# Meta-token keys as a full 128-row tile, and the output products of an RWKV chunk ordered by array tile

## The chip, the cores and the metric

The kernel runs on one core of one Trainium2 chip. The metric is the time of one execution on the device in microseconds (us). TensorE is called PE here, its weight loads PEld; VectorE is DVE, ScalarE is ACT, GpSimd is POOL, SyncE is SP. "Granted clock" is the share of TensorE's full speed (2.4 GHz) that the records show; it is either 1.0 or 0.5 (1.2 GHz) at any moment.

## The reference, cut to what matters

A one-layer decoder trunk over 1024 tokens with 16 learned "meta" tokens in front (1040 positions). One projection feeds four mixers; their outputs are concatenated, projected and normalised, and a mixture of 16 experts follows. The change touches three of the mixers' parts:

```python
# A: sliding window, 4 heads: the keys are the 16 meta tokens, the block before, the own block
kpos = jnp.concatenate([meta positions 0..15, qpos - BLOCK, qpos], axis=1)
p = jax.nn.softmax(jnp.concatenate([s, sink], axis=-1), axis=-1)[..., :-1]
o = jnp.einsum('bnhgqk,bnkhd->bnqhgd', p, vw)
# B: differential attention, 4 heads, causal over all earlier positions (meta tokens too)
attn = p[:, :, 0] - lam * p[:, :, 1]
o = jnp.einsum('bhqk,bkhd->bqhd', attn, vp)
# C: RWKV-7, a state S of 64x64 per head, 4 heads, 1040 steps
S = S * w_t + sa * (kk_t * a_t) + v_t * k_t        # outer products
y_t = S @ r_t
```

Meta tokens are dropped from the output, so attention is computed for 8 blocks of 128 queries. Blocks of keys begin at position 16, and the 16 meta keys stand alone in front.

## The kernel before, in words

The whole kernel is one program in float32 (some products as pairs of float32r halves). After a stage for the input norm and the first projections (to about 320 us of the profile), one long stage holds the rest of the projections, the RWKV recurrence and both attentions (about 320 to 735 us); then come the output projection with norm and routing (to about 900 us) and the experts.

In the long stage nothing is ordered by hand. Each piece of work is a step, `add(engine, cost, function, deps, priority, take, use)`, with an estimated cost in us; `Steps.run` (line 145) takes, again and again, the step that could start first by these estimates (ties by priority), and calls its function, which writes the instructions. The order in which the steps are called is the order of each engine's queue; an engine works through its queue strictly in that order. `take` and `use` stand for slots in rings of buffers (two PSUM tiles "tp", two score tiles "sc", two tiles "at" and so on).

RWKV is cut into 17 chunks of 64 positions (one pad chunk part). `chain(i)` (line 1038) holds the serial part. For each chunk: `f1` (state times input, L1056), `g1` (L1079), `h1` (new state, L1095), and `y1` (L1112 to 1116), which makes the chunk's outputs: for 2 tiles of channels `ct` and 2 halves `par` it adds two products into the same 64x64 piece of PSUM, one of the old state with a 64x64 array tile (`w.s0[q, ct]`, L1115) and one of 128 rows with a 128x64 array tile (`o.bz[:, par, 1, j]`, L1116). A float32 product is two instructions, so `y1` is 16 instructions. It runs for chunks 1 to 16. `y2` copies the result out on ACT.

The value rows live in `vs` (9 blocks of 128 rows, three groups of 128 columns); block 0 holds the 16 meta rows in partitions 0 to 15, its other partitions are never written or read. `values` (L1259) loads and transposes them; `switch` (L1234) closes the projections' buffers and opens the pool in which `vs` lies.

Sliding-window attention, `swa(kv, i)` (L1339), runs 2 x 8 times, each for two heads `g`: scores, minimum, exponential, transposes of the probabilities of the near blocks (`t1`, L1383), of the 16 meta columns (`t3`, L1391), copies to `at` (ACT L1386; DVE L1394), then the products `p1`: for each `g` the near blocks (L1403, 128 rows) and the meta block (L1404, 16 rows). Differential attention, `diff(h, i)` (L1423), runs 4 x 8 times: the key blocks stand in the order 1 to i+1, then 0, in groups of four; each group is transposed (`t1`, L1522), the full blocks are copied by ACT (`t2`, L1525), the 16-row meta block by DVE (`t3`, L1528); then `p1` multiplies the full blocks (L1542) and the meta block (L1543). `p2_` (L1407, L1546) scales the result out of PSUM.

Of the kernel before, what the change touches and what calls it, by code (L numbers as in the profile page):

```python
# [13 lines left out]
AF = mybir.ActivationFunctionType  # L14
# [5 lines left out]
P = 128  # L20
# [4 lines left out]
M = 16  # L25
NT = S + M
C = 64
# [167 lines left out]
def build(tc, A, out, dbg=None, upto=99):  # L195
# [62 lines left out]
    add = sA.add  # L258
# [10 lines left out]
    o = 0  # L269
# [531 lines left out]
    small = {}  # L801
# [236 lines left out]
    def chain(i):  # L1038
        o = grp[i]
        add = st_.add  # L1040
        p2 = lambda t: t.rearrange("p (a c) -> p a c", c=C)
        for ci, c in enumerate(o.chunks):
            pr = PRG(i)
            four = [(ct, par, HALF[par], HALF[1 - par], ct * o.nc + ci) for ct in range(2) for par in range(2)]
            w = O()
            _, sdone, sslot = state
            rd = None
            sps_dep = []
            if c > 0:
                ss_, sr, sp_ = Slot("ca"), Slot("r"), Slot("sp0")  # L1050

                def f1(w=w, ci=ci, four=four):
                    w.s0 = state[0]
                    w.r = rt("r", [2, C])
                    for ct, par, q, r, j in four:
                        T.matmul(small["ca"][q, ct * C:(ct + 1) * C], o.ab[q, ct, ci, 0], w.s0[q, ct], start=True, stop=True)  # L1056

                def f2(w=w, ci=ci):
                    V.tensor_tensor(w.r, p2(small["ca"]), o.lv[:, :, ci], op=ALU.add)

                def f3(w=w, c=c):
                    w.sp0 = rt("sp0", [2, C])
                    for ct in range(2):
                        G.tensor_scalar(w.sp0[:, ct], w.s0[:, ct], pend[:, ct, c:c + 1], None, op0=ALU.mult)
                a = add("PE", .25, f1, [sdone, o.loaded], pr, take=[ss_, sr], use=[sslot, o.slot])
                rd = add("DVE", dve(P), f2, [a, o.lvd], pr, use=[ss_, sr, o.slv])
                if c < NCH - 1:
                    sps_dep = [add("Pool", 2 * pol(C), f3, [a], pr, take=[sp_], use=[sslot])]
            else:
                sr = o.slv  # L1070

                def f2(w=w, ci=ci):
                    w.r = o.lv[:, :, ci]
                rd = add("DVE", 0, f2, [o.lvd], pr)
            scs = Slot("cs")

            def g1(w=w, four=four):
                for ct, par, q, r, j in four:
                    T.matmul(small["cs"][q, ct * C:(ct + 1) * C], o.X[q, j], w.r[q, ct], start=True, stop=True)  # L1079

            def g2(ci=ci):
                ACT.activation(o.bz[HALF[0], 0, 1, ci::o.nc], p2(small["cs"])[HALF[0]], AF.Copy)

            def g3(ci=ci):
                V.tensor_copy(o.bz[HALF[1], 1, 1, ci::o.nc], p2(small["cs"])[HALF[1]])
            a = add("PE", .25, g1, [rd, o.Xd], pr, take=[scs], use=[sr, o.sX])
            sad = [add("ACT", act(P), g2, [a] + o.bzd, pr, use=[scs, o.sbz]), add("DVE", dve(P), g3, [a] + o.bzd, pr, use=[scs, o.sbz])]
            s0slot = sslot
            if c < NCH - 1:
                sh, ns = Slot("cp"), Slot("s1")  # L1090

                def h1(w=w, four=four):
                    w.s1 = rt("s1", [2, C])
                    for ct, par, q, r, j in four:
                        T.matmul(small["cp"][q, ct * C:(ct + 1) * C], o.bz[:, par, 0, j], o.bz[:, par, 1, j], start=True, stop=True)  # L1095

                def h2(w=w, c=c):
                    s1_ = w.s1
                    for ct in range(2):
                        d, pe_ = small["cp"][:, ct * C:(ct + 1) * C], pend[:, ct, c:c + 1]  # L1100
                        if c > 0:
                            V.scalar_tensor_tensor(s1_[:, ct], d, pe_, w.sp0[:, ct], op0=ALU.mult, op1=ALU.add)
                        else:
                            V.tensor_scalar(s1_[:, ct], d, pe_, None, op0=ALU.mult)
                    state[0] = s1_
                a = add("PE", .43, h1, sad, pr, take=[sh, ns], use=[o.sbz])
                state[1] = add("DVE", 2 * dve(C), h2, [a] + sps_dep, pr, use=[sh, ns] + ([sp_] if c > 0 else []))
                state[2] = ns
            if c > 0:
                sy = Slot("cy")  # L1110

                def y1(w=w, ci=ci, four=four):  # L1112
                    for ct, par, q, r, j in four:
                        d = small["cy"][q, ct * C:(ct + 1) * C]
                        T.matmul(d, w.s0[q, ct], o.ab[q, ct, ci, 1], start=True, stop=False)  # L1115
                        T.matmul(d, o.bz[:, par, 1, j], o.gs[:, par, j, C:2 * C], start=False, stop=True)  # L1116

                def y2(c=c):
                    ACT.activation(MX[:, 4:6, (c - 1) * C:c * C], p2(small["cy"]), AF.Copy)
                a = add("PE", .7, y1, sad, pr + .05, take=[sy], use=[s0slot, o.slot, o.sbz, o.sgs])  # L1120
                ydone[c] = add("ACT", act(P), y2, [a], pr + .05, use=[sy])
# [137 lines left out]
    def values(i, pr, deps):  # L1259
# [8 lines left out]
        for j0 in (0, 4, 8):  # L1268
            j1 = min(j0 + 4, 9)
            lo = max(j0, 1)  # L1270
            sl = Slot("tp")
            v = O()

            def t1(v=v, j0=j0, j1=j1):
                v.tb = bank2("tp")
                for j in range(j0, j1):
                    a, n = (0, M) if j == 0 else (M + P * (j - 1), P)
                    T.transpose(v.tb[:n, (j - j0) * P:(j - j0 + 1) * P], w.t[:, 0, a:a + n], ident)

            def t2(v=v, j0=j0, j1=j1, lo=lo):  # L1280
                ACT.activation(vs[:, lo:j1, i * P:(i + 1) * P],
                               v.tb.rearrange("p (a c) -> p a c", c=P)[:, lo - j0:j1 - j0], AF.Copy)
                if j0 == 0:
                    ACT.activation(vs[:M, 0, i * P:(i + 1) * P], v.tb[:M, :P], AF.Copy)
            a = st_.add("PE", .45, t1, [l], pr, take=[sl], use=[se])
            out.append(st_.add("ACT", act(512), t2, [a], pr, use=[sl]))
# [52 lines left out]
    def swa(kv, i, pr, tabs, vals):  # L1339
# [48 lines left out]
        def t3():  # L1388
            w.tm = bank2("tp")
            for g in range(2):  # L1390
                T.transpose(w.tm[:M, g * P:(g + 1) * P], w.E[:, g, 0:M], ident)  # L1391

        def t4():
            V.tensor_copy(fl(w.at[:M, 4:6]), w.tm[:M, :2 * P])  # L1394

        def p1():
            w.po = bank2("tp")
# [2 lines left out]
            for g in range(2):  # L1400
                o = w.po[:, P * g:P * g + P]
                for z in range(n):
                    T.matmul(o, w.at[:, g * n + z], vs[:, i + 1 if n == 1 else i + z, vc], start=(z == 0), stop=False)  # L1403
                T.matmul(o, w.at[:M, 4 + g], vs[:M, 0, vc], start=False, stop=True)  # L1404

        def p2_():
            V.tensor_tensor(out_tile(kv)[:, i].rearrange("p (a b) -> p a b", b=64), w.po[:, :2 * P].rearrange("p (a b) -> p a b", b=P)[:, :, 64 * kv:64 * kv + 64],  # L1407
# [15 lines left out]
    def diff(h, i, pr, tabs, vals):  # L1423
# [81 lines left out]
            cb = add("Pool", 2 * pol(W), c3, [r], pr, use=[sE])  # L1505
        else:
            cb = add("DVE", dve(W), c2, [r], pr, use=[sE])
        blocks = list(range(1, i + 2)) + [0]
        last = []
        for b0 in range(0, len(blocks), 4):  # L1510
            bl = blocks[b0:b0 + 4]
            full = [j for j in bl if j]
            stt = Slot("tp")
            v = O()

            def t1(v=v, bl=bl, b0=b0):
# [1 line left out]
                if b0 == 0:  # L1518
                    w.at = at_("at", [9, P])
                for z, j in enumerate(bl):  # L1520
                    a_, n_ = (M + P * (j - 1), P) if j else (0, M)
                    T.transpose(v.tb[:n_, z * P:(z + 1) * P], w.E[:, 0, a_:a_ + n_], ident)  # L1522

            def t2(v=v, full=full):
                ACT.activation(fl(w.at[:, full[0]:full[-1] + 1]), v.tb[:, :len(full) * P], AF.Copy)  # L1525

            def t3(v=v, z=len(bl) - 1):
                V.tensor_copy(w.at[:M, 0], v.tb[:M, z * P:(z + 1) * P])  # L1528
            a = add("PE", .11 * len(bl), t1, [cb], pr, take=[stt] + ([] if b0 else [sat]), use=[sE] + ([sat] if b0 else []))
            inorder("t", a)  # L1530
            if full:
                last.append(add("ACT", act(128 * len(full)), t2, [a], pr, use=[stt, sat]))
            if 0 in bl:
                last.append(add("DVE", dve(128), t3, [a] + last[:1], pr, use=[stt, sat]))

        def p1():
            w.po = bank2("tp")
            out_tile(2 + hp_)
            o = w.po[:, :P]
            vc = slice(P + P * hp_, 2 * P + P * hp_)  # L1540
            for j in range(1, i + 2):
                T.matmul(o, w.at[:, j], vs[:, j, vc], start=(j == 1), stop=False)  # L1542
            T.matmul(o, w.at[:M, 0], vs[:M, 0, vc], start=False, stop=True)  # L1543

        def p2_():
            ACT.activation(out_tile(2 + hp_)[:, i, 64 * hh_:64 * hh_ + 64], w.po[:, 64 * hh_:64 * hh_ + 64], AF.Copy, scale=w.rs[:, 0:1])  # L1546
# [59 lines left out]
    for ct in range(2):  # L1606
# [3 lines left out]
        for q, w in enumerate(cw_):  # L1610
            conv_silu(ct, q, w, last)
    sw = [st_.add("SY", 0, switch, sp_, 0)]
    load_qk(0, sw)
    tabs = [st_.add("SY", 6, tables, after, 30)]
    tabs = [st_.add("DVE", 1.6, far_bias, tabs, 5)]
# [796 lines left out]
```

## Time and profile before

| what | value |
|---|---|
| median of 3 runs | 1461.32 us (1460.78 to 1466.42) |
| the profiled execution: its time, its span | 1463.69 us, 1461.8 us |
| mean granted TensorE clock | 0.908 |
| PE busy, share of the span | 1286.5 us, 88% |
| DVE busy | 913.9 us, 63% |
| ACT busy | 623.7 us, 43% |
| POOL busy | 279.2 us, 19% |

The page counts an engine as busy while any of its instructions runs; matmuls are pipelined, so a busy PE may still be slow at what it does. How long a matmul really holds PE is read from the time between the starts of neighbours in the timeline, not from its own duration. The span is divided into stretches by what runs in them, and each stretch has its own limit.

### The profile page before, as it was taken

The numbers are of one execution on the slowest core, as the hardware profiler recorded it, in microseconds if no ns is written. First come the engines' busy times: TensorE is split into PE (matmuls) and PEld (weight loads), VectorE is DVE, ScalarE is ACT, GpSimd is POOL, SyncE is SP. The second block draws the span as 40 slices with busy tenths as digits, with TensorE's granted clock in tenths as the row PEclk, the third lists the DMA queues.
The fourth block names the chain that finished last, engine by engine and source line by source line (L and its number), as shares of the span: only waits on it lengthen the run. The fifth ranks groups of instructions, "written<-read, shape, count | busy, mean of one in ns | idle before, by whom it ended". The sixth has DMA issues, their size and how long they took to land. (4 is left out here: it accounts for less than half of the span.)

```text
span 1461.8 us, 22362 instructions
## 1 busy us (share of the span) xinstructions
PE 1286.5 (88%) x8095; PEld 1041.1 (71%) x8095; DVE 913.9 (63%) x1713; ACT 623.7 (43%) x1101; POOL 279.2 (19%) x252
## 2 busy tenths in 40 slices
PE   5998899999989999889879986799899899889960
PEld 4896898887767688767557765677677678677750
DVE  7556649983234657557468776747754882875275
ACT  6353212233133445336643224636643771764151
POOL 3522213331102022132100113111121211111100
PEclk9999999999957989959779996999999999999995
DMA  8214337221360220400143265978966994996452
GB/s 200 78 45 134 128 106 213 86 74 59 77 162 19 69 69 21 98 23 1 58 135 138 101 182 186 298 238 245 350 183 186 357 338 137 278 335 174 138 175 116
DMA packets 165465, 219.65 MB, mean 150 GB/s; under 512 B 36046, under 2 KB 134490, under 8 KB 165036
## 3 DMA queue, kind: packets, MB, share of 16 engines
q1 hardware_dynamic: 156604, 188.66, 40.5%
q0 software_dynamic: 8688, 28.87, 8.2%
q8 instruction: 86, 1.41, 0.4%
q14 instruction: 87, 0.71, 0.1%
HBM read 174.38 MB, written 45.46 MB: 150 GB/s over the span
## 5 line engine op out<-in xcount | busy, mean ns | idle before, releaser
L454 PE MATMUL acc<-hh,wh 128*128 128x256 f32 (+2 forms) x288 | 97.1, 338 | 0.0
L454 PE MATMUL acc<-hh,wl 128*128 128x256 f32 (+2 forms) x288 | 93.2, 325 | 0.0
L2124 PE MATMUL rw<-wh,at 128*128 128x512 f32 x224 | 83.8, 424 | 8.4 <-ACT at L2099 5.8
L1180 DVE SCALAR_TENSOR_TENSOR CY<-MX,cvw,CY 128x1024 f32<-128x1024 f32 x60 | 87.9, 1485 | 0.1
L454 PE MATMUL acc<-hl,wh 128*128 128x256 f32 (+2 forms) x288 | 87.7, 323 | 0.0
L1668 DVE TENSOR_TENSOR wl<-MX,wh 128x1024 fp32r<-128x1024 f32 x66 | 78.4, 1221 | 12.1 <-ACT wh L1664 9.4
L2128 POOL DMA_INDIRECT acc__132<-y,ixs x21 | 40.9, 1948 | 183.8 <-issue 58.7
L1668 DVE TENSOR_TENSOR wol<-MX,woh 128x1024 fp32r<-128x1024 f32 x51 | 60.8, 1222 | 18.5 <-ACT woh L1664 12.3
L1664 ACT ACTIVATE wh<-MX 128x1024 fp32r<-128x1024 f32 x66 | 66.8, 1051 | 9.4 <-DMA MX<-in_exp_w_dram 6.9
L1478 ACT ACTIVATE E<-sc,nm 128x144 f32<-128x144 f32 (+7 forms) x64 | 47.9, 750 | 42.4 <-DVE nm L1472 31.2
L454 PEld LDWEIGHTS acc<-hh,wh 128*128 128x128 f32 x288 | 55.6, 193 | 5.7 <-issue 5.2
L1502 POOL TENSOR_TENSOR E<-E,rho 128x272 f32<-128x272 f32 (+3 forms) x16 | 20.8, 1298 | 197.9 <-DVE rho L1496 118.4
L2124 PEld LDWEIGHTS rw<-wh,at 128*128 128x128 f32 x224 | 44.0, 198 | 19.8 <-ACT at L2099 6.7
L1826 PE MATMUL oacc<-woh,mh 128*128 128x512 f32 x128 | 55.1, 430 | 1.8 <-ACT woh L1778 1.7
L1664 ACT ACTIVATE woh<-MX 128x1024 fp32r<-128x1024 f32 x51 | 51.9, 1050 | 10.4 <-DMA MX<-in_exp_w_dram 7.1
L454 PEld LDWEIGHTS acc<-hh,wl 128*128 128x128 f32 x288 | 55.3, 192 | 1.3 <-issue 1.0
L2100 DVE TENSOR_TENSOR xte<-acc,xte 128x512 fp32r<-128x512 f32 x44 | 28.6, 686 | 40.4 <-ACT xte L2099 40.4
L1826 PE MATMUL oacc<-wol,mh 128*128 128x512 f32 x128 | 52.3, 408 | 1.5 <-DVE wol L1781 1.5
L454 PEld LDWEIGHTS acc<-hl,wh 128*128 128x128 f32 x288 | 53.6, 189 | 0.0
L1826 PE MATMUL oacc<-woh,ml 128*128 128x512 f32 x128 | 52.0, 406 | 0.0
L2119 DVE TENSOR_TENSOR act<-act,acc 128x256 f32<-128x256 f32 x31 | 13.0, 421 | 57.9 <-ACT act L2118 57.0
L2099 ACT ACTIVATE xte<-acc 128x512 fp32r<-128x512 f32 x44 | 24.3, 596 | 57.1 <-PE acc L2097 26.1
(474 smaller groups left out, 3576.2 us busy)
## 6 DMA issues: line engine op xcount, KB each, us to landing
MX<-in_exp_w_dram SPq DMA_DIRECT2D x192, 256.0 KB
MX<-in_exp_w_dram SPq DMA_DIRECT2D x48, 512.0 KB
CY<-in_exp_w_dram SPq DMA_DIRECT2D x64, 256.0 KB
raw<-in_w_in_dram SPq DMA_DIRECT2D x20, 512.0 KB
qk<-dqk SPq DMA_DIRECT2D x64, 130.0 KB
CY<-in_exp_w_dram SPq DMA_DIRECT2D x16, 512.0 KB
dab<-ab SPq DMA_DIRECT2D x2, 2176.0 KB
qk<-dqk SPq DMA_DIRECT2D x16, 260.0 KB
```

The lines of the kernel that those rows point to most:

```text
L454: T.matmul(v.acc[:, :wid], wt[:, k], x[:, k, c0:c0 + wid], start=(z + y == 0 and wt is w.h), stop=(z + y == len(ks) - 1))
L1180: V.scalar_tensor_tensor(y, hc[:, M + j:M + j + S], cvw[:, ct, j:j + 1], y, op0=ALU.mult, op1=ALU.add)
L1478: ACT.activation(w.E[:, c, off:W], w.sc[c][:, :W - off], AF.Exp, bias=w.nm[:, c:c + 1], scale=-1.0, accum_out=w.s[:, c:c + 1])
L1502: G.tensor_tensor(w.E[:, 1, :W], w.E[:, 1, :W], w.rho.to_broadcast([P, W]), op=ALU.mult)
L1664: ACT.activation(slot_h[i % HLS][0], raw[i], AF.Copy)
L1668: eng.tensor_tensor(l, raw[i], h.bitcast(F32), op=ALU.subtract)
L1826: T.matmul(v.o, x_[:, k], y_[k][:, 512 * n:512 * n + 512], start=(i == 0 and j == 0), stop=False)
L2099: ACT.activation(dst[:, 0, s], tb[:, :m * P], AF.Copy)
L2100: V.tensor_tensor(dst[:, 1, s], tb[:, :m * P], dst[:, 0, s].bitcast(F32), op=ALU.subtract)
L2119: V.tensor_tensor(s, s, a[:, 256:512], op=ALU.mult)
L2124: T.matmul(o[n], at[:, x, k * P:(k + 1) * P], w[k][y][:, n * 512:n * 512 + 512], start=(k == 0 and (x, y) == (0, 0)), stop=(k == 3 and x = ...
L2128: G.indirect_dma_start(out=acc_, out_offset=bass.IndirectOffsetOnAxis(ap=ix[:, 0:1], axis=0), in_=y, in_offset=None, compute_op=ALU.add)
```

## The change

Three edits, one idea in each.

1. The meta keys are treated like any other block of 128 keys. The transposes take columns 0 to 127 of the scores in place of 0 to 15, all 128 rows are copied to `at`, and the products run over 128 rows of `vs[:, 0]`. One new DVE step, after `switch`, sets `vs[:, 0]` to zero, so that rows 16 to 127 (which hold probabilities of keys 0 to 111 of block 1) add nothing.
2. In `diff` the block order becomes 0 to i+1. The DVE copy `t3` goes; ACT's `t2` copies all blocks of a group. The number of groups is the same as before; for i = 3 and 7 the last group is one full block copied by ACT, where it was the meta block copied by DVE.
3. In `y1` the eight products are reordered: the two 128x64 ones of `ct` 0, then the two 64x64 ones of `ct` 0, the two 64x64 ones of `ct` 1, and the two 128x64 ones of `ct` 1.

```diff
@@ chain, y1
-                    for ct, par, q, r, j in four:
-                        d = small["cy"][q, ct * C:(ct + 1) * C]
-                        T.matmul(d, w.s0[q, ct], o.ab[q, ct, ci, 1], start=True, stop=False)
-                        T.matmul(d, o.bz[:, par, 1, j], o.gs[:, par, j, C:2 * C], start=False, stop=True)
+                    for ct in range(2):
+                        for k in (ct, 1 - ct):
+                            for _, par, q, r, j in four[2 * ct:2 * ct + 2]:
+                                d = small["cy"][q, ct * C:(ct + 1) * C]
+                                if k:
+                                    T.matmul(d, w.s0[q, ct], o.ab[q, ct, ci, 1], start=(k == ct), stop=(k != ct))
+                                else:
+                                    T.matmul(d, o.bz[:, par, 1, j], o.gs[:, par, j, C:2 * C], start=(k == ct), stop=(k != ct))
@@ swa
-                T.transpose(w.tm[:M, g * P:(g + 1) * P], w.E[:, g, 0:M], ident)
+                T.transpose(w.tm[:, g * P:(g + 1) * P], w.E[:, g, 0:P], ident)
-            V.tensor_copy(fl(w.at[:M, 4:6]), w.tm[:M, :2 * P])
+            V.tensor_copy(fl(w.at[:, 4:6]), w.tm[:, :2 * P])
-                T.matmul(o, w.at[:M, 4 + g], vs[:M, 0, vc], start=False, stop=True)
+                T.matmul(o, w.at[:, 4 + g], vs[:, 0, vc], start=False, stop=True)
@@ diff
-        blocks = list(range(1, i + 2)) + [0]
+        blocks = list(range(i + 2))
-            def t2(v=v, full=full):
-                ACT.activation(fl(w.at[:, full[0]:full[-1] + 1]), v.tb[:, :len(full) * P], AF.Copy)
-            def t3(v=v, z=len(bl) - 1):
-                V.tensor_copy(w.at[:M, 0], v.tb[:M, z * P:(z + 1) * P])
+            def t2(v=v, bl=bl):
+                ACT.activation(fl(w.at[:, bl[0]:bl[-1] + 1]), v.tb[:, :len(bl) * P], AF.Copy)
-            if full:
-                last.append(add("ACT", act(128 * len(full)), t2, [a], pr, use=[stt, sat]))
-            if 0 in bl:
-                last.append(add("DVE", dve(128), t3, [a] + last[:1], pr, use=[stt, sat]))
+            last.append(add("ACT", act(128 * len(bl)), t2, [a], pr, use=[stt, sat]))
-            for j in range(1, i + 2):
-                T.matmul(o, w.at[:, j], vs[:, j, vc], start=(j == 1), stop=False)
-            T.matmul(o, w.at[:M, 0], vs[:M, 0, vc], start=False, stop=True)
+            for j in blocks:
+                T.matmul(o, w.at[:, j], vs[:, j, vc], start=(j == 0), stop=(j == blocks[-1]))
@@ after switch
+    sw.append(st_.add("DVE", .3, lambda: V.memset(vs[:, 0], 0.0), sw, 0.5))
```

## Rows read from the trace of the kernel before

**Rows 1.** Page, part 1: busy time of each engine

```profile
PE 1286.5 (88%) x8095; PEld 1041.1 (71%) x8095; DVE 913.9 (63%) x1713; ACT 623.7 (43%) x1101; POOL 279.2 (19%) x252
```

**Rows 2.** Windows: stretch, length, busy us of PE, PEld, DVE, ACT, POOL, clock, DMA

```profile
320.00:394.00 74.00, 72.12 (x760) 59.01 (x759) 28.42 (x62) 19.43 (x37) 12.96 (x14) 1.00 0.15 50
394.00:422.00 28.00, 23.80 (x205) 18.34 (x207) 6.10 (x21) 9.62 (x28) 3.15 (x6) 0.64 0.94 233
422.00:735.00 313.00, 289.67 (x2466) 224.61 (x2463) 183.23 (x587) 146.53 (x388) 63.65 (x60) 0.84 0.18 45
735.00:900.00 165.00, 139.21 (x668) 106.05 (x667) 122.87 (x326) 55.36 (x79) 20.76 (x20) 0.86 0.45 149
```

**Rows 3.** Waits of PE, 422 to 735 us: total, times, longest

```profile
PE prep L993 <- DVE um L1017: 7.1, 3, 3.7
PE tp L1542 <- DVE at L1528: 2.1, 2, 1.7
```

**Rows 4.** Timeline of PE, full clock: start, us, line, out<-in, array tile, operands

```profile
586.02 0.45 PE L1056 MATMUL chain<-s,abv 64*64 64x64 f32 x8
586.40 0.66 PE L1522 MATMUL tp<-c__63,E 128*128 128x128 f32 x4
...
588.87 0.45 PE L1095 MATMUL chain<-bz 128*64 128x64 f32 x8
589.25 0.33 PE L1115 MATMUL chain<-abv,s 64*64 64x64 f32 x2
589.51 0.33 PE L1116 MATMUL chain<-gs,bz 128*64 128x64 f32 x2
...
591.31 0.73 PE L1460 MATMUL sc<-qk,qk 128*128 128x512 f32 x2
```

**Rows 5.** Timeline of PE at half clock, the same work

```profile
637.33 0.70 PE L1095 MATMUL chain<-bz 128*64 128x64 f32 x8 [0.60 <-DVE bz L1085]
637.96 0.47 PE L1115 MATMUL chain<-abv,s 64*64 64x64 f32 x2
...
641.18 0.69 PE L983 MATMUL prep<-c__63,abv 64*128 64x64 f32 x4
```

**Rows 6.** Windows of line L1116 alone: stretch, length, PE, PEld, clock, DMA

```profile
320.00:394.00 74.00, 5.26 (x32) 3.06 (x32) 1.00 0.15 50
394.00:422.00 28.00, 3.21 (x16) 1.91 (x16) 0.64 0.94 233
422.00:735.00 313.00, 15.94 (x80) 9.45 (x80) 0.84 0.18 45
```

**Rows 7.** Timeline of PE, full clock, attention products and a meta transpose

```profile
488.36 0.61 PE L1403 MATMUL tp<-vs,at 128*128 128x128 f32 x4
...
490.36 0.66 PE L1522 MATMUL tp<-c__63,E 128*128 128x128 f32 x4
...
493.90 1.28 PE L1542 MATMUL tp<-vs,at 128*128 128x128 f32 x10
495.11 0.48 PE L1543 MATMUL tp<-vs,at 16*128 16x128 f32 x2
495.53 0.68 PE L993 MATMUL prep<-X,um 64*64 64x64 f32 x16
496.14 0.39 PE L1391 MATMUL tp<-c__63,Es 128*16 128x128 f32 x2
496.36 0.60 PE L1522 MATMUL tp<-c__63,E 128*128 128x128 f32 x4
```

**Rows 8.** Groups by line, 420 to 735 us: count | busy us, mean ns | idle before

```profile
L1543 PE MATMUL tp<-vs,at 16*128 16x128 f32 x64 | 16.7, 343 | 0.0
...
L1528 DVE COPY at<-tp 16x128 f32<-16x128 f32 x32 | 8.8, 274 | 5.7 <-ACT at L1525 3.9 <-PE tp L1522 1.8
```

**Rows 9.** Groups by line and shape, ACT, 422 to 735 us

```profile
L1525 ACT ACTIVATE at<-tp 128x128 f32<-128x128 f32 x8 | 2.2, 273 | 2.6 <-PE tp L1522 2.5
```

**Rows 10.** Timeline of PE at the switch to attention

```profile
408.64 1.86 PE L1278 MATMUL tp<-c__63,E 128*16 128x128 f32 x8 [1.64 <-DMA E<-dvv]
```

More of the change, by code (lines that the diff above doesn't have):

```diff
@@ L1276, in t1 @@
                 for j in range(j0, j1):
-                    a, n = (0, M) if j == 0 else (M + P * (j - 1), P)
+                    a, n = (0, P) if j == 0 else (M + P * (j - 1), P)
                     T.transpose(v.tb[:n, (j - j0) * P:(j - j0 + 1) * P], w.t[:, 0, a:a + n], ident)
@@ L1511, in diff @@
             bl = blocks[b0:b0 + 4]
-            full = [j for j in bl if j]
             stt = Slot("tp")
@@ L1520, in t1 @@
                 for z, j in enumerate(bl):
-                    a_, n_ = (M + P * (j - 1), P) if j else (0, M)
-                    T.transpose(v.tb[:n_, z * P:(z + 1) * P], w.E[:, 0, a_:a_ + n_], ident)
-            def t2(v=v, full=full):
-                ACT.activation(fl(w.at[:, full[0]:full[-1] + 1]), v.tb[:, :len(full) * P], AF.Copy)
-            def t3(v=v, z=len(bl) - 1):
-                V.tensor_copy(w.at[:M, 0], v.tb[:M, z * P:(z + 1) * P])
+                    a_ = M + P * (j - 1) if j else 0
+                    T.transpose(v.tb[:, z * P:(z + 1) * P], w.E[:, 0, a_:a_ + P], ident)
+            def t2(v=v, bl=bl):
+                ACT.activation(fl(w.at[:, bl[0]:bl[-1] + 1]), v.tb[:, :len(bl) * P], AF.Copy)
             a = add("PE", .11 * len(bl), t1, [cb], pr, take=[stt] + ([] if b0 else [sat]), use=[sE] + ([sat] if b0 else []))
             inorder("t", a)
-            if full:
-                last.append(add("ACT", act(128 * len(full)), t2, [a], pr, use=[stt, sat]))
-            if 0 in bl:
-                last.append(add("DVE", dve(128), t3, [a] + last[:1], pr, use=[stt, sat]))
+            last.append(add("ACT", act(128 * len(bl)), t2, [a], pr, use=[stt, sat]))
         def p1():
```

## Prediction

> **What bounds the kernel now.** I read the page first: PE is busy 88% of the span, the next engine, DVE, 63% [rows 1]. That is an average over stages, so I cut the span into stretches. The edits touch only work between 320 and 735 us, and there PE is busy 72 of 74, 24 of 28 and 290 of 313 us, while DVE has 183 and ACT 147 of the last 313 [rows 2]. So PE bounds the stretch; what ends its idle time is read next, and it is little: the 23 us of idle from 422 to 735 are scattered, the largest single cause is 7.1 us in 3 waits [rows 3]. The middle stretch, 394 to 422, is different: DMA is at 0.94 of its engines, DVE works 6 of 28 us [rows 2], and PE waits for the value loads [rows 10]. Busy does not mean well used: the timeline shows how far apart PE's instructions start, and that is what the change alters. The granted clock is at its lower level for part of the stage (mean 0.84 from 422 on, 1.00 before 394 [rows 2]).
>
> **The change part by part.**
>
> **RWKV's outputs.** At full clock one y1 holds PE from 589.25 to 591.31: 2.06 us for 16 instructions, as eight pairs of 0.26 that alternate between a 64x64 and a 128x64 array tile [rows 4]. The same kinds of product, eight in a row on one kind of tile and going back and forth between its two halves, take 0.38 us with the step to the next kind: L1095 for the 128x64 kind (588.87 to 589.25), L1056 for the 64x64 kind (586.02 to 586.40) [rows 4]. So a pair in a row costs 0.095 and a pair in alternation 0.26; 0.16 is then the most that a change of tile can cost. The new order is four 128x64 instructions, eight 64x64, four 128x64: two such bursts, 0.76, plus one more change, 0.16, in all 0.92. It saves 1.14 us per chunk. At half clock the same rows give 3.22 us for y1 (637.96 to 641.18) and 0.63 for the burst of eight (637.33 to 637.96) [rows 5]; a pair alternating is 0.40, in a row 0.16, so the new order takes 1.26 + 0.24 = 1.50 and saves 1.72.
> Where the 16 chunks lie: 8 instructions of L1116 each, so 32, 16 and 80 records are 4, 2 and 10 chunks [rows 6]. The first four run at full clock: 4.6 us. The last ten take 0.199 us busy per record, against 0.164 in the first four and 0.200 in the middle two, where both levels of clock occur [rows 6]; I take half of the ten at each level: 14.3 us. The middle two would save 2.9 us, but PE there waits for the value loads afterwards [rows 10], so it would only wait longer; I count nothing.
>
> **Products over the meta block.** A sliding-window p1 holds PE from 488.36 to 490.36, 2.00 us for 12 instructions, four of them on 16 rows [rows 7]. Twelve ordinary ones cost 12 times 0.11 to 0.12: ten of L1542 take 1.21 us (493.90 to 495.11), and that already holds the step to the 16-row tile [rows 7]. New time 1.32 to 1.45, saving 0.55 to 0.68; over 16 tasks 9 to 11 us. A differential p1 goes from 493.90 to 495.53, 1.63 for 12, so 0.18 to 0.31 is saved where the next instruction changes the tile anyway (here a 64x64 burst); 32 tasks, as 64 records of L1543 show [rows 8], give 6 to 10. Where a full tile follows, the sliding-window rows say more (0.3 per pair), so I take the upper ends: 20 us together, all after 422.
> A rule speaks against this term. The Trainium skill, page "TensorE: Matmul & The Clock Gate", section "Why this matters for your kernels", says that a single product over 32 rows takes as long as one over 128, and gains only when several run at once. By it the 16-row pairs would cost no more than full ones and the 20 us would be nothing; the rows disagree, since the 16-row pair with its way out takes 0.42 (495.11 to 495.53) where two ordinary ones take 0.24 [rows 7]. I sum by the rows, and keep the rule as a rival.
>
> **Transposes and copies.** The 16-column transposes become 128 columns wide. A pair of them starts 0.22 us before its follower (496.14 to 496.36), 0.11 each, no less than full instructions [rows 7], so I count 0 and at most 0.05 each on 67 of them, 3 us, as the other end. DVE loses 32 copies of 0.274, 8.8 us [rows 8]. ACT gets them as wider copies; a copy of 128 columns alone is 0.273 [rows 9], so at most 8.7 us, on an engine that idles for more than half of the stretch. Two PE waits of 2.1 us that the DVE copy ended [rows 3] go, because the products then wait for ACT alone: 2.1 us, or nothing if ACT is late by as much.
>
> **The memset.** One DVE step of 128x384, not in the trace; its ends are 0.27 (the DVE copy of rows 8) and three times the ACT copy of rows 9, 0.8; I take 0.3. It waits until the projections' buffers are free, and behind it in DVE's queue stand RWKV steps for which PE waits; ahead of it in time is the load of values, and DVE has 22 of 28 us idle there [rows 2]. Hidden; 0.8 us if not.
>
> **The sum.** Early stretch: 4.6 us of PE time in a stretch 97% busy; I let 4.1 pass. Late stretch: 14.3 + 20 = 34 us less work for PE out of 290. Not all can pass: the order of each queue is fixed, and when PE comes earlier it meets steps of DVE and ACT that are not done; the 23 us that it idles now will grow. Neither engine is near its limit (59% and 47%), so I take 65%, 22 us; the ends are 30% (10 us, the saved time mostly becoming waits) and 100%. With 2.1 for the removed hop the sum is 28 us. After 735 all work begins from the attention outputs and from buffers that they free (DMA share 0.18 before, 0.45 after [rows 2]), so I let the shift pass to the end. The profiled execution took 1463.69 us (span 1461.8 and 1.9 around it), 2.4 above the median; 1463.7 - 28 = 1436 by it, and 1433 from the median. I forecast **1434.5**.
>
> **The rivals.**
>
> *Everything passes, and the clock gains.* All 41 us (4.6 + 34 + 2.1) go, and denser work leaves fewer stretches at half clock: 1420 and, with some 8 us of clock, 1412. For it: PE is 93% busy. Against: the scattered waits. I put it at 1416.
>
> *The saved time becomes waits.* The planner also orders anew, since the costs it sees change on ACT and DVE and a step is added; a worse order costs waits like the 3.7 us one of rows 3. With 30% passing, 10 + 4 less 2 for a worse order: 1451. For it: the stage is a web of three engines with two buffers for most things.
>
> *The reorder gives nothing.* If the two halves did not overlap because both kinds add into the same columns of PSUM, y1 would stay near 2 us: 0.65 x 20 + 2.1 = 15, 1448. Against: L1056 and L1095 show the overlap on the same tiles.
>
> *The 16-row products give nothing (the rule named above).* 4.1 + 0.65 x 14.3 + 2.1 = 15.5, 1448. Rows 7 speak against it.
>
> *Slower: the clock falls.* Place: 422 to 735. The mean clock of 0.84 says that 32%, 100 us, run at half speed. New gaps could bring more; half speed stretches the work by 1.56 (y1: 3.22 to 2.06) to 1.66 (the burst: 0.63 to 0.38), so each further us at half that stands for full-speed work costs about 0.4. It takes back the 28 us from 70 more us at half, that is when the stretch's mean clock falls to about 0.70; at 0.64 or so, with 105 more, the kernel is slower: 1476. For it: the stretch from 620 on is at half clock though PE is busy. Against: the change takes out idle array time, not work.
>
> **How the numbers follow.** Chances: forecast 0.58; everything passes 0.11; waits 0.17; reorder nothing 0.05; 16 rows nothing 0.04; slower 0.05. A 0.5% difference, 7.3 us, is about what a measurement of this kernel can tell from no change: the border is 1454. The forecast and its three lesser forms lie below it, the waits case with 0.09 below and 0.08 above. So faster 0.87, same 0.08, slower 0.05. The range: 28 us is worked out from 65% with ends at 30% and 100%; 1417 to 1452 holds the forecast, the two half-gains, half of the waits case and half of the full gain.
>
> **What would show it.** In the profile after: y1 at 0.8 to 0.95 us at full clock and about 1.5 at half; a sliding-window p1 near 1.4 us; no instruction with 16 rows on PE; L1528 gone and ACT's copies 4 to 9 us longer in sum; the first four chunks' gain before 394; a longer wait of PE at the value loads; the end of attention 25 to 30 us earlier, with PE idle in 422 to 735 grown from 23 to some 35 us, and the stage after of the same length. The prediction is wrong if y1's pairs do not start together, if the idle time grows by 30 us or more, or if the mean clock of the stretch moves by more than 0.05.

## The result and the profile after

The changed kernel takes **1410.13 us** (median of 6 runs, 1408.35 to 1412.4), the kernel before 1461.05 us beside it (6 runs, 1457.58 to 1467.85): a ratio of **0.9646, 95% interval 0.9618 to 0.9674**, 51 us less. The forecast was 1434.5 with a range from 1417 to 1452; the direction was right, the size was not: 28 us were forecast, and the result lies 7 us below the range. Among the experiments below, three runs of e7, one of e12 and two of the kernel before lie over 1.5% above the fastest of their kernel; they count in the medians, but not in ratios, half-clock times and ranges of times or clocks.

The profiled execution took 1411.35 us, with a span of 1409.5 and a mean granted clock of 0.927 (0.908 before). Page of after, part 1:

```profile
PE 1221.4 (87%) x8095; PEld 1006.0 (71%) x8095; DVE 908.9 (64%) x1682; ACT 627.2 (44%) x1109; POOL 278.5 (20%) x252
```

PE issues the same 8095 instructions as before [rows 1] and is busy 65 us less. Windows of after, cut at about the same marks of the work as the windows of before [rows 2], with the same columns:

```profile
320.00:390.00 70.00, 66.79 (x753) 55.43 (x754) 29.92 (x63) 19.31 (x37) 12.99 (x14) 1.00 0.17 52
390.00:416.00 26.00, 17.80 (x224) 14.40 (x218) 6.06 (x21) 9.41 (x28) 3.13 (x6) 0.74 0.94 226
416.00:686.00 270.00, 240.29 (x2463) 200.25 (x2459) 178.37 (x558) 150.94 (x398) 62.58 (x61) 0.90 0.22 55
686.00:850.00 164.00, 137.83 (x677) 106.60 (x678) 122.60 (x324) 55.27 (x78) 20.76 (x21) 0.89 0.47 152
```

The attention stretch shrank from 313 to 270 us. PE's idle time in it grew from 23.3 to 29.7 us, and its mean clock rose from 0.84 to 0.90: 54 us at half clock, where it was 100. The last product of the projections starts at 389.5 (393.1 before), the first of the output projection at 693.7 (744.9), the first of the experts at 844.3 (896.7): nearly the whole gain is made before the output projection, and the stages behind it keep their lengths and pass it on. Timeline of PE in after at full clock: the new y1 [rows 4], the wait for the value loads [rows 10], and two sets of attention products [rows 7]; columns start, us, line, tiles, array tile, operands:

```profile
393.72 0.45 PE L1095 MATMUL chain<-bz 128*64 128x64 f32 x8
394.00 0.29 PE L1120 MATMUL chain<-gs,bz 128*64 128x64 f32 x4
394.22 0.45 PE L1118 MATMUL chain<-abv,s 64*64 64x64 f32 x8
394.59 0.34 PE L1120 MATMUL chain<-gs,bz 128*64 128x64 f32 x4
394.86 0.96 PE L966 MATMUL prep<-c__63,vch 64*64 64x64 f32 x16
...
405.27 1.94 PE L1282 MATMUL tp<-c__63,E 128*128 128x128 f32 x8 [5.40 <-DMA E<-dvv]
...
578.54 0.61 PE L1407 MATMUL tp<-vs,at 128*128 128x128 f32 x4
578.99 0.39 PE L1408 MATMUL tp<-vs,at 128*128 128x128 f32 x2
579.22 0.61 PE L1407 MATMUL tp<-vs,at 128*128 128x128 f32 x4
579.66 0.39 PE L1408 MATMUL tp<-vs,at 128*128 128x128 f32 x2
579.88 0.60 PE L1525 MATMUL tp<-c__63,E 128*128 128x128 f32 x4
...
581.52 1.95 PE L1539 MATMUL tp<-vs,at 128*128 128x128 f32 x16
583.31 0.38 PE L1395 MATMUL tp<-c__63,Es 128*128 128x128 f32 x2
```

y1 holds PE from 394.00 to 394.86, 0.86 us (2.06 before). A sliding-window p1 goes from 578.54 to 579.88, 1.34 us (2.00 before); 16 instructions of a differential p1 take 1.79 us (581.52 to 583.31), 0.112 each. Every meta instruction is now a full tile. The wait at the value loads grew from 1.64 to 5.40 us. Waits of PE in after, 416 to 686 us (total, times, longest), and, by line, ACT's copies and DVE's new memset:

```profile
PE prep L993 <- DVE um L1017: 9.2, 5, 4.2
PE tp L1395 <- ACT sq L1154: 2.8, 1, 2.8
PE sc L1464 <- ACT E L1482: 2.5, 2, 1.7
...
L1528 ACT ACTIVATE at<-tp 128x512 f32<-128x512 f32 (+3 forms) x56 | 27.6, 505 | 28.1 <-PE tp L1525 27.6 <-ACT es L1376 0.3
...
L1609 DVE MEMSET vs<- 128x384 f32 x1 | 0.4, 378 | 0.0
```

The wait on DVE's copy [rows 3] is gone, the largest cause left is the same as before (L993 on `um`).

**Where the time went, by the trace.** I gave every moment from the first score product to the first output-projection product to one of four sums: from the start of each PE instruction to the start of the next (or to its own end, where PE then idles), by kind, and idle.

| us | before | after | change | forecast |
|---|---|---|---|---|
| length of this stage | 333.8 | 285.3 | -48.5 | -24 |
| y1 | 26.2 | 8.9 | -17.3 | -14.3 |
| attention products p1 | 88.4 | 66.7 | -21.7 | -20 |
| **all other PE work** | 189.1 | 173.0 | **-16.1** | 0 |
| PE idle | 30.1 | 36.6 | +6.5 | +10 (12 less the removed hop) |
| of all this at half clock | 122.2 | 63.4 | -58.8 | none |

The row that the forecast didn't have is the fourth. These instructions are the same in both kernels, apart from the wider meta transposes; what differs is the clock at which they run: 78 us of them were at half clock before, 43 after. Part of the rows above it is the clock's too: y1 was at half clock for 15 of its 26 us before and for 0.2 us after, p1 for 13 and 8 us.

### The profile page after: what moved, and what is told of

It reads as the page before. It is cut to its first block, busy times and chain, and to the rows that moved or that the text cites. A ratio compares the mean times of both kernels' runs of the same rounds, so it can differ in the third digit from the quotient of the medians.

```text
span 1409.5 us, 22368 instructions
## 1 busy us (share of the span) xinstructions
PE 1221.4 (87%) x8095; PEld 1006.0 (71%) x8095; DVE 908.9 (64%) x1682; ACT 627.2 (44%) x1109; POOL 278.5 (20%) x252
## 5 line engine op out<-in xcount | busy, mean ns | idle before, releaser
L1539 PE MATMUL tp<-vs,at 128*128 128x128 f32 x352 | 48.8, 290 | 0.6 <-ACT at L1528 0.3
L2096 ACT ACTIVATE at<-tp 128x256 fp32r<-128x256 f32 x46 | 17.6, 382 | 70.8 <-PE tp L2094 56.4
```

Of the source, the lines that this page charges most:

```text
L1539: T.matmul(o, w.at[:, j], vs[:, j, vc], start=(j == 0), stop=(j == blocks[-1]))
L2096: ACT.activation(dst[:, 0, s], tb[:, :m * P], AF.Copy)
```

## The experiments

Three theories stand against each other. **Work:** the time goes with the PE time that is taken out, and the clock is chance. **Clock:** the alternating and 16-row products also pull the granted clock down, so that other work gets faster when they go. **Plan:** the planner, whose costs changed, found a better order.

A figure that all experiments need: the records give each run's mean granted clock, and since a moment is at 1.0 or 0.5, the time at half clock is 2 x (1 - mean) x time. The kernel before spread by 16 to 21 us on each of three chips, and its time goes with this figure: 43 runs with 216 to 270 us at half clock lie on the line 1454.2 + 0.40 x (half-clock time - 239.6), with 2.1 us of scatter about it and a standard error of 0.024 on the slope. So a run of another kernel can be compared with before at equal half-clock time: what is left is **work**, and 0.40 us for each us at half clock is **clock**. Where a kernel's half-clock time lies outside 216 to 270 us, as in after (198), the line is drawn on beyond its runs, and the split is an estimate. (The prediction had worked out "about 0.4" from [rows 4, 5].)

| kernel | median us | ratio, 95% interval | half-clock us (before, same chip) | against the line |
|---|---|---|---|---|
| after | 1410.1 | 0.9646 [0.9618, 0.9674] | 198 (-) | -27.4 |
| after, second chip (e13) | 1411.6 | 0.9690 [0.9639, 0.9741] | 197 (245) | -26.8 |
| e1, y1 alone | 1427.5 | 0.9838 [0.9794, 0.9883] | 213 (234) | -15.8 |
| e2, 128 rows alone | 1435.0 | 0.9881 [0.9844, 0.9918] | 222 (234) | -14.7 |
| e3, both, old order of queues | 1411.0 | 0.9707 [0.9665, 0.9749] | 202 (234) | -29.4 |
| e5, e1 + 4 full-tile products | 1442.0 | 0.9917 [0.9884, 0.9949] | 205 (234) | +2.6 |
| e7, e1 + 4 small alternating ones | 1447.4 | 0.9954 [0.9916, 0.9992] | 226 (235) | -3.1 |
| e10, before + 4 full-tile products | 1463.2 | 1.0105 [1.0041, 1.0168] | 224 (235) | +16.0 |
| e11, e1 + 8 full-tile products | 1453.7 | 0.9975 [0.9939, 1.0011] | 195 (245) | +16.8 |
| e12, e1 + 8 small alternating ones | 1467.0 | 1.0107 [1.0052, 1.0163] | 239 (245) | +11.7 |
| e8, after + whole-tile transposes | 1411.5 | 0.9744 [0.9689, 0.9800] | 194 (235) | -23.9 |
| e14, after, planner groups by tile | 1464.9 | 1.0067 [1.0035, 1.0100] | 301 (245) | -13.9 |

For the six runs of before beside after, half-clock times aren't listed; their median of 1461.05 stands at 257 us on the line. Every ratio is against runs of before on the same chip; half-clock times and distances from the line are means over the runs.

**One edit at a time, and both in the old order.** e1 is the kernel before with edit 3 alone.

> The kernel before with the reordered y1 alone; the queues' order is that of before. Work theory (the gain is PE time taken out, the granted clock only a bystander): 4.1 + 0.65 to 0.8 of 14.3 = 13 to 16 us, about 1446. Clock theory (about 20 us of the 51 come from less time at half clock; the attention stage of the changed kernel has 63 us at half, of before 122): 10 us more, about 1436, with the half-clock time of that stage at 90 or less.

Measured 1427.49 us, 0.9838. At full clock the new y1 takes 0.86 us; at half clock, timeline of PE in e1:

```profile
611.09 0.70 PE L1095 MATMUL chain<-bz 128*64 128x64 f32 x8 [0.60 <-DVE bz L1085]
611.58 0.43 PE L1120 MATMUL chain<-gs,bz 128*64 128x64 f32 x4
611.93 0.69 PE L1118 MATMUL chain<-abv,s 64*64 64x64 f32 x8
612.55 0.48 PE L1120 MATMUL chain<-gs,bz 128*64 128x64 f32 x4
612.97 0.69 PE L983 MATMUL prep<-c__63,abv 64*128 64x64 f32 x4
```

1.39 us (611.58 to 612.97), where it was 3.22 [rows 5]. e2 is the meta block on 128 rows, with the block order, the DVE copy and y1 of before; the memset is written inside `switch`, as no step of its own:

```diff
+            V.memset(vs[:, 0], 0.0)
...
-  a_, n_ = (M + P * (j - 1), P) if j else (0, M)
+  a_, n_ = (M + P * (j - 1), P) if j else (0, P)
...
-  V.tensor_copy(w.at[:M, 0], v.tb[:M, z * P:(z + 1) * P])
+  V.tensor_copy(w.at[:, 0], v.tb[:, z * P:(z + 1) * P])
...
-  T.matmul(o, w.at[:M, 0], vs[:M, 0, vc], start=False, stop=True)
+  T.matmul(o, w.at[:, 0], vs[:, 0, vc], start=False, stop=True)
...
```

> The kernel before with the meta block on 128 rows (zero value rows, wide transposes and products) but the block order, the DVE copy and the queues' order of before; y1 as before. Work theory: 0.65 to 0.8 of 20 = 13 to 16 us, about 1446. Clock theory: 10 us more, about 1436, and the half-clock time falls by 30 us. If 16-row products cost no more than 128-row ones: 1461.

Measured 1435.03 us, 0.9881. e3 has both diffs and so no step, cost or dependency that the planner sees changes.

> Both of these together, still in the queues' order of before, with the meta copy on DVE. If the new order of the queues and the move of the copy to ACT brought the part of the gain that was not forecast (plan theory): 1425 to 1433, 15 to 23 us above the changed kernel. If they did not: 1410 to 1415.

Measured 1410.98 us, 0.9707. The theory of the plan falls: with the queues in their old order the kernel is as fast as after (1411.57 on another chip, e13). The two edits add up: 26 and 18 us below the chip's median of before make 44, and e3 is 42 below. Against the line they are worth 15.8 and 14.7 us of work; each also lowers the half-clock time of its runs, by 21 and 12 us, and both together by 32. e1's gain of 26 us is what the clock theory expected (10 us above the 13 to 16 of the work theory); e2's 18 us lie between the two theories, and its half-clock time fell by 12 us, not by the 30 expected.

**Work or clock.** If the drop of half-clock time comes from the small-tile alternation itself, then PE time put back in another form should not bring it back. e5 puts back y1's old PE time as four full-tile products whose result y1 then overwrites (the edit is shown against e1).

```diff
 def y1(w=w, ci=ci, four=four):
+    for z in range(4):
+        T.matmul(small["cy"], fl(o.ab[:, z % 2, ci, 2:4]), fl(o.ab[:, z // 2, ci, 0:2]), start=True, stop=True)
     for ct in range(2):
```

> The reordered y1 as in the first, with four full-tile products (8 instructions, about 0.9 us at full clock, and one or two changes of tile more) put ahead of it into the same PSUM columns, where the first real product overwrites them: PE is held about as long as by y1 before, but by full-tile work. Work theory: 1457 to 1464, no gain. Clock theory (time in which the array stands between tiles is what the clock answers to): half-clock time falls as in the first run, and 8 to 15 us are gained, about 1450.

Timeline of PE in e5, one chunk:

```profile
573.50 1.16 PE L1114 MATMUL chain<-abv 128*128 128x128 f32 x8
574.58 0.34 PE L1122 MATMUL chain<-gs,bz 128*64 128x64 f32 x4
574.85 0.45 PE L1120 MATMUL chain<-abv,s 64*64 64x64 f32 x8
575.23 0.34 PE L1122 MATMUL chain<-gs,bz 128*64 128x64 f32 x4
575.49 0.71 PE L1409 MATMUL tp<-vs,at 128*128 128x128 f32 x4
```

The block holds PE for 1.99 us (573.50 to 575.49), where y1 of before held it for 2.06. Work alone says no gain. Measured 1442.04 us, 0.9917: 11 us faster than before with the same PE time per chunk. The half-clock time is 205 us against 234; 0.40 x 29 = 11.6 us, as much as the whole gain. e7 puts in alternating small products instead, the kind that y1 had:

```diff
+    for z in range(4):
+        _, par, q, r, j = four[z]
+        d = small["cy"][q, (z % 2) * C:(z % 2 + 1) * C]
+        if z % 2:
+            T.matmul(d, o.bz[:, par, 1, j], o.gs[:, par, j, C:2 * C], start=True, stop=True)
+        else:
+            T.matmul(d, w.s0[q, z // 2], o.ab[q, z // 2, ci, 1], start=True, stop=True)
```

> The reordered y1 with four small products ahead of it that alternate between a 64x64 and a 128x64 array tile (into the same PSUM columns, overwritten): PE is held about as long as with the four full-tile ones of the run before, and as by y1 before, but again by changes of tile. Work theory: the same as with the full-tile filler, 0.99 of before. Clock theory: as before, ratio 0.997 to 1.003, with as much half-clock time as a profile of before has.

Measured 1447.35 us, 0.9954. Its block is 0.2 us shorter than that of e5, and by work it is the cheaper one (-3.1 against +2.6), yet it gains less against before. But the two intervals overlap, so this pair alone decides nothing. I doubled both fillers: e11 is e5 with eight full-tile products, e12 is e7 with eight small ones, on one chip.

> The reordered y1 with eight full-tile products (16 instructions, 1.8 us at full clock) ahead of it, into the same PSUM columns, overwritten. With four of them y1 held PE for 2.00 us at full clock (before: 2.05); with eight it will be 2.9. Work theory: 16 times 0.84 us more than before, 13 us, some 12 of them passing, ratio 1.008. Clock theory (full-tile work keeps the clock up): granted clock of the runs 0.93 as with four, and no more than 2 us slower than before, ratio 0.995 to 1.002.

> The same with eight small products that alternate between a 64x64 and a 128x64 array tile: y1 will hold PE for 2.8 us at full clock, 0.1 less than with the eight full-tile ones. Work theory: 1 to 2 us faster than the full-tile filler. Clock theory: granted clock of the runs 0.92 or less, as before or under it, and 8 us or more slower than the full-tile filler, ratio to before 1.006 or more.

Timeline of PE, the block in e11:

```profile
576.25 2.05 PE L1114 MATMUL chain<-abv 128*128 128x128 f32 x16
578.23 0.33 PE L1122 MATMUL chain<-gs,bz 128*64 128x64 f32 x4
578.50 0.45 PE L1120 MATMUL chain<-abv,s 64*64 64x64 f32 x8
578.88 0.34 PE L1122 MATMUL chain<-gs,bz 128*64 128x64 f32 x4
579.14 0.71 PE L1409 MATMUL tp<-vs,at 128*128 128x128 f32 x4
```

and in e12 (L1119 and L1117 are the filler; the rows between alternate in the same way):

```profile
573.83 0.33 PE L1119 MATMUL chain<-abv,s 64*64 64x64 f32 x2
574.09 0.33 PE L1117 MATMUL chain<-gs,bz 128*64 128x64 f32 x2
...
576.00 0.45 PE L1125 MATMUL chain<-abv,s 64*64 64x64 f32 x8
576.38 0.34 PE L1127 MATMUL chain<-gs,bz 128*64 128x64 f32 x4
576.65 0.60 PE L1414 MATMUL tp<-vs,at 128*128 128x128 f32 x3
```

2.89 us (576.25 to 579.14) with the full tiles, 2.82 (573.83 to 576.65) with the small ones. At half clock, too, the full-tile block is the longer one: 5.16 us in e11 (635.44 to 640.60), 4.47 in e12 (633.07 to 637.54). Measured: e11 1453.68 us, 0.9975; e12 1467.03, 1.0107. The one that holds PE longer is 13 us faster (so too by the means of the runs in the ratios, 1453.0 and 1465.9), and the intervals of the ratios are apart. Its runs had clocks of 0.925 to 0.941, those of e12 0.911 to 0.924, those of before on this chip 0.908 to 0.924. So with PE equally occupied, the kind of work sets how long the lower clock lasts: half-clock time fell by 29 and 50 us with full-tile filler, by 9 and 5 with small alternating filler. With more full-tile filler it fell further: by 21 us in e1, which has none, by 29 in e5 (not clear of the spread of e1's runs), by 50 in e11. The single profiled executions don't show this by themselves: the attention stage of e5 and e7 has 82.6 and 83.0 us at half clock, that of e11 and e12 69.7 and 71.8, so the verdict rests on the runs. e6 is the kernel before again, to see how far one profile can be read.

> The kernel before, unchanged, for a second profile: the times of before spread from 1442 to 1468, so its half-clock time in the attention stage may be no fixed number. Clock theory: a time between 1442 and 1468 with a half-clock time that goes with it, 0.4 us of time per us at half, so 70 us at half for 1442 and 122 for 1463. Work theory: the spread is elsewhere, and the half-clock time is 115 to 125 again.

Measured 1463.54 us at a clock of 0.911; the stage is again 122.0 us at half clock (before 122.2), which both theories allow at this time, and the window of 422 to 735 is nearly the same as in [rows 2]:

```profile
422.00:735.00 313.00, 289.60 (x2448) 223.57 (x2446) 183.93 (x587) 147.62 (x389) 63.69 (x60) 0.83 0.18 44
```

Both profiles of before come from runs above its medians on three chips (1451 to 1456), so the profiles of before and after stand further apart than typical runs of the two do. e10 asks the reverse: if full-tile work raises the clock, does adding it to the kernel before, ahead of the old y1, pay? The diff is that of e5, on the old order.

> The kernel before with the four full-tile products put ahead of its old y1, nothing else changed: PE gets 16 times 1.1 us more to do (more at half clock), 18 to 20 us, and no change of tile goes. Work theory: 15 to 18 us slower, ratio 1.011. Clock theory (full-tile work keeps the clock up): half-clock time falls by some 30 us, and only 3 to 8 us slower, ratio 1.003 to 1.005.

Measured 1463.15 us, 1.0105. It doesn't: this is the ratio that the work theory expected. The half-clock time fell by 11 us, not by 30, worth 4.4, and the added work cost 16. Added full-tile work costs more than its clock gives back here; what paid was to have less of the other.

**After again.** e13 is the changed kernel, unaltered, on a second chip.

> The changed kernel again, on the chip of these runs, as a measure for the next one and of its spread: 1405 to 1415, granted clock 0.925 to 0.935. Its ratio here tells how much of the first 0.9646 was the luck of before's clock: 0.965 to 0.975.

Measured 1411.57 us against 1456.0 for before, 0.969. After is the same on both chips to 1.5 us; before isn't. Of the 51 us of the first comparison 5 are the slower runs of before there (1461 against 1456 us), which the line puts at 12 us more at half clock; 44 us is the gain on this chip.

**Two attempts to go further.** The input transposes of the RWKV part (L983 in after) are 68 instructions on a 64x128 tile; e8 makes them 34 on the full tile, by taking the channel tile `ct` in place of the half `par` as the unit:

```diff
+    T.transpose(small["pu"][:, ci * P:(ci + 1) * P], fl(o.ab[:, ct, ci, 2:4]), ident)
...
+    ACT.activation(o.bz[:, :, 0, ct * nc_:(ct + 1) * nc_],
+                   small["pu"].rearrange("p (j a c) -> p a j c", a=2, c=C)[:, :, :nc_], AF.Copy)
```

> The changed kernel, and one more piece of work put on the full tile: the transposes of each group's input columns (18 bursts of four on a 64x128 tile) become 18 bursts of two 128x128 ones, which hold both halves at once; steps, costs and the queues' order are those of the changed kernel. Work theory: 0.2 us of each burst and up to 0.1 per change of tile, 18 times, 4 to 5 us of PE, 3 to 4 of them passing: ratio to before about 0.003 lower than the changed kernel's. Clock theory: the same, or a little more.

Measured 1411.5 us, 0.9744. No gain over after is seen. The projections' end came 2 us earlier (387.3), but the attention stage was 286.5 us long against 285.3: what came earlier was waited for later. e14 lets the planner see the price of a change of array tile, so that it groups steps of one kind (each RWKV step gets a label of its tile, all other steps share one, and 0.1 us is added to a PE step's start where its label differs from that of the last):

```diff
+SWITCH = .1
...
+                if s.eng == "PE" and getattr(s, "kind", "f") != last:
+                    t += SWITCH
```

> The changed kernel with a planner that knows the cost of a change of array tile: a PE step of another tile kind than the one before it is taken as if it started 0.1 us later. All instructions the same, their order another. If changes of tile are the waste that the rows show, bursts of one kind come together and the attention stage loses some 30 changes of 0.1 us: 2 to 5 us faster than the changed kernel. If the new order makes waits instead: equal or slower.

Measured 1464.88 us, 1.0067: slower than after by 53 us, all of its gain and more. The order of the stage changed widely. Window of e14 from 320 to 735 us, and waits of PE in it:

```profile
320.00:735.00 415.00, 345.95 (x3717) 290.76 (x3716) 216.89 (x670) 175.45 (x464) 78.50 (x93) 0.83 0.22 56
...
PE prep L1001 <- DVE um L1026: 11.3, 16, 1.6
PE tp L1297 <- issue: 7.7, 1, 7.7
PE prep L972 <- DVE X L1033: 7.3, 6, 2.4
```

From 320 us to the output projection PE idles 75.8 us (47.7 in after) and spends 149.8 at half clock (72.8). In its runs the half-clock time is 104 us above e13's, which at 0.40 is 42 us; against the line it has 13 us less of work gain left. By that account most of the loss goes with the clock, and the rest is waits; the figure of 301 lies outside the 216 to 270 us of which the line is made, so the split is rough. Which of the two, the waits or the small bursts gathered together, brought the clock down isn't separated by this run.

## Why the prediction was wrong

The steps in the prediction's order:

- **What bounds the stage:** right. Less PE time in 320 to 735 us is less time to the end, and the stages behind only move.
- **y1:** right in kind, slightly low in size. 0.92 and 1.50 us forecast, 0.86 and 1.39 measured. The pairs of a run start nearly together, so the rival "the reorder gives nothing" falls; e1 alone gives 1.6%. The term of the late stage was 14.3 and measured 17.3: the 3 us more are the clock's. Before, the ten chunks took 2.62 us each, as assumed (half at 2.06, half at 3.22: 2.64). After, they took 0.89 each, because 0.2 of their 8.9 us were at half clock, where the sum had left half of the ten chunks there, at 1.50.
- **Products on 128 rows:** 20 forecast, 21.7 measured, of which some 2 are the clock's (5 us less at half clock, at 0.40). The rule that I kept as a rival fell. The Trainium skill, page "TensorE: Matmul & The Clock Gate", section "Why this matters for your kernels", has a single product over 32 rows take as long as one over 128. Here the rows disagree: at full clock the second instruction of a 16-row pair started 0.21 us after the first (median over L1543), that of a full pair 0.11 (L1542), and e2 is 1.2% faster.
- **Transposes, copies, memset, removed hop:** as forecast. ACT's copies under L1528 took 27.6 us where those of L1525 took 23.3 before, 4.3 more (4 to 9 forecast), the memset 0.38 (0.3 forecast) and hidden, the wait on the DVE copy gone.
- **The early and middle stretches:** the projections end 3.6 us earlier (4.1 forecast). In the middle the wait at the value loads took what came earlier, as forecast (1.64 to 5.40); the first score product is 2.7 us earlier.
- **The share that passes, 65%:** as a figure for work it held. At equal half-clock time after is 27 us below before, and the sum was 28. By its parts, 4.1 + 0.65 x 14.3 = 13.4 for y1 stands against 15.8 in e1, and 0.65 x 20 + 2.1 = 15.1 for the rows against 14.7 in e2. From 320 us to the output projection PE idles 12.2 us more (35.5 to 47.7), the 12 that I allowed, though half of it fell before attention.
- **The clock: the step that failed.** The sum is priced at the clock of the profile before and has no term for a change of clock; only two rivals had one. The half-clock time of whole runs fell from 257 us (by the line) to 198: 0.40 x 59 = 24 us. 27 + 24 = 51, but this sum closes of itself, since the 257 was read off the line. The two profiles, each with its own clock, say the same without that reading: 268 us of the execution at half clock before, 205 after, 63 us less, which is 25 us at 0.40. On the chip of e13 it is 26.8 and 0.40 x 48 = 19, together 46 against the 44 measured.

The rival "everything passes, and the clock gains" gave 1412 to 1416 with a chance of 0.11. Its time was right, its terms were not: it had 41 us of work passing and 8 of clock, and the runs show 27 and 24. The rival that the saved time becomes waits fell (idle grew by 12, not by 24), and so did that of a falling clock, whose sign was wrong: I had argued that new gaps could bring more half-clock time, and gave no weight to the kind of work that filled PE before. The reason written against it, that the change "takes out idle array time, not work", was the hint. (Its border was off as well: 70 us more at half clock make 170 of 313, a mean clock of 0.73, where it says 0.70.) The prediction also named a mean clock of the stretch moved by more than 0.05 as what would prove it wrong; it moved by 0.06.

Shown by e5, e11 and e12: at equal PE time, products on the full tile leave less time at half clock than alternating products on small tiles. Between e11 and e12 the difference is 45 us of half-clock time, 18 us by the line; 13 of them show, because the small filler is 5 us cheaper as work. e5 and e7 point the same way (21 us of half-clock time) without deciding it. Not tested: whether the 16-row products act on the clock in the same way; e2's half-clock time fell by 12 us, but no run gives that PE time back in another form. Only argued: why. In y1 the tile changes, the array is partly empty, and the engine stands still between pairs, all at once, and no run separates these. Nor was it tried whether a run of small products without a change of tile lowers the clock as well; y1 in its new order is nearly such a run, and e1's half-clock time fell by 21 us, but with less PE time as well.

## What to carry to other kernels

Where PE is the bound, look at the distance between the starts of its instructions: products that alternate between array tiles, or use a few rows of it, can be put in one run per tile or padded with zeros to the full tile, without touching the order of the queues (e3). Price such a change in two terms, the PE time and the time at half clock, each us of which cost 0.40 us here; get the second from several runs of the kernel before and their clocks, since one profile shows one of them. But measure before you regroup the steps of a web of engines to save changes of tile (the one try, e14, lost all of the gain), or add work to hold the clock up (e10 lost 1%).

## What the runs showed of the hardware that was not expected

- **The clock's share in the spread of one kernel.** The runs of before lie between 1442 and 1468 us at clocks of 0.925 to 0.908, and the clock accounts for all but 2.1 us of scatter.
- **The price of small tiles.** 16 instructions of y1 took 2.06 us as alternating pairs and 0.86 as three runs. The Trainium skill, page "TensorEngine Tiling (Array Packing)", section "Key Properties", says that changing the tiling mode drains the engine; the trace fits that: five of the seven changes of tile inside y1 went, and 1.2 us with them. How much of that is the change itself and how much the two halves of a tile now side by side, these runs don't separate.
- **A busy PE does not keep its clock.** With eight small alternating products more per chunk (e12) the clock of the runs was no higher than before (0.911 to 0.924, beside 0.908 to 0.924), with eight full-tile ones (e11) it was 0.925 to 0.941.
